# Odd mixer of a two-block transformer kernel: attention values as two float32r passes per head, softmax division moved to ScalarE, query and key tiles projected pair by pair

## The chip, the cores and the metric

The kernel runs on one core of a Trainium2 chip. The metric is the device time of one execution in microseconds. The kernel before was run three times; its median is 1922.75 us (1922.05 to 1923.62).

## What is computed

The reference takes 512 tokens of width 1024 in float32 through two blocks: a differential attention with a mixture of experts, and then an even mixer, a gated FFN, an odd mixer, a second FFN and a last norm. The change is almost all in the odd mixer:

```python
def odd_mixer(xn, w_in, w_out, forget_b, sinks, rope_h):
    qc, kc, vc, fc, qd, kd, vd = _split(xn @ w_in, ODD_SPLITS)
    log_f = jax.nn.log_sigmoid(fc + forget_b)
    yc = forgetting_attention(heads(qc, 8), heads(kc, 8), heads(vc, 8), log_f)
    yd = sink_window_gqa(apply_rope(heads(qd, 8)), apply_rope(heads(kd, 2)), heads(vd, 2), sinks)
    return jnp.concatenate([yc, yd], -1) @ w_out
```

`forgetting_attention` is causal softmax attention with 8 heads of 64, whose logits get the difference of a cumulated log forget gate. `sink_window_gqa` lets each block of 128 queries see its own and the previous block, with 8 query heads on 2 value heads, and a learned sink in the denominator.

## The kernel before, in words

The whole program stands in one class with a method per stage; the odd mixer is `stage_e` (L937 to L1118). All matrices lie in 128 partitions. A weight product in near-full precision is three float32r matmuls: `split` makes a high part on ScalarE (L110) and a low part on VectorE (L111), and `mm3` issues high by high, high by low and low by high (L135 to L137, or L139 to L141 where the activations are the stationary operand). In profile and order, these are `mm<-...`. `fm` makes a projection with tokens along the free axis, `tm` one with tokens on the partitions.

`stage_e` first projects part 1 of the values (`v_units(1)`, 324 columns), then `kd` and four tiles `qd` with rotary embedding, and then runs two series of heads, four query blocks each:

- **window heads** (`w_score`, `w_turn`, `w_value`): scores `s` (two passes), bias and minimum on VectorE (L1065), Exp on ScalarE (L1067), Exp of the sink (L1068), sum and reciprocal, division on VectorE (L1071), transposes `t` on TensorE (L1080), two copies from PSUM on ScalarE (L1083, L1084), values `pv` (L1095).
- **forgetting heads** (`soft_heads`, L681 on, shared with the even mixer): scores (L694), bias and minimum (L697), Exp (L698), reciprocal (L699), division (L700), transposes (L709), one copy of the turned block (L711), and at a head's last block its four value matmuls (L721).

The value matmuls take float32 on both sides: 64 columns of values are stationary, the turned weights move. Two heads write the two halves of one PSUM bank, and `y_out` (L740) splits the bank into high and low for the output projection (L743, L744). PSUM holds four banks for `mm`, two for `s` (`ns`), one for `t` (`ntp`) and one for `pv` (`npv`).

A unit of the window series issues the score of a block, the turn of the block two before and the value of the one four before. `weave` sets these units between those of a projection: the window heads beside `qc`, `kc` and part 0 of the values, the forgetting heads beside the second half of the output projection (`mm<-ydh`, `mm<-ydl`). The first half (`mm<-ych`, `mm<-ycl`) follows. `prep(c)` makes stacked high and low parts of the queries and keys of heads 2c and 2c+1 (`nh`, `nl`, then about a dozen DMAs on SP's queue), and is asked for two heads ahead. The tile framework's scheduler then sets the order on each engine.

Of the kernel before, what the change touches and what calls it, by code (L numbers as in the profile page):

```python
# [23 lines left out]
SOFT, ATT, WIN = (2, 4), (1, 4), (2, 4)  # L24
# [57 lines left out]
class K:  # L82
# [598 lines left out]
    def soft_heads(self, pool, heads, begin):  # L681


        nc = self.nc
        sbs, pts, pvs = {}, {}, {}

        def score(u, i):
            hd = heads[u]
            if i == 0:
# [12 lines left out]
        def turn(u, i):  # L702
            n = P * (i + 1)
            if i == 0:
                pts[u] = pool.tile([P, 13, P], F32, name="ptall", tag="ptall", bufs=2)
# [5 lines left out]
            nc.scalar.copy(pts[u][:, i:4 * i + 1:3], tp[:, :n].rearrange("p (a b) -> p a b", b=P))  # L711

        def value(u, i):
            if i != NT - 1:
                return
            e = u % 2
            if e == 0:
                pvs[u // 2] = self.pvt()
            pv, pt = pvs[u // 2], pts.pop(u)
            for j in range(NT):  # L720
                nc.tensor.matmul(pv[64 * e:64 * e + 64, j * P:], lhsT=heads[u]["v"](j), rhs=pt[:, 4 * j:3 * j + 4],  # L721
                                 start=j == 0, stop=j == NT - 1, skip_group_check=True)
            if e == 1:
                heads[u]["done"](u // 2, pvs.pop(u // 2))

        us = [(u, i) for u in range(len(heads)) for i in range(NT)]
        units = []
        for t in range(len(us) + SOFT[1]):
            parts = [(f, us[t - d], c) for f, d, c in ((score, 0, 0.11), (turn, SOFT[0], 0.11), (value, SOFT[1], 0.3))
                     if 0 <= t - d < len(us)]  # L730

            def fn(parts=parts, t=t):
                if t == 0:
                    begin()
# [3 lines left out]
        return units  # L738

# [8 lines left out]
    def stage_c(self):  # L748
# [4 lines left out]
        with tc.tile_pool(name="pc", bufs=1) as pc:  # L753
# [167 lines left out]
            def head(kind, hh, v, begin, bias, y):  # L921
                def qk(i, n):
                    q, *k = stacks[kind, hh]
                    return [(q[:, i * P:(i + 1) * P], t[:, :n]) for t in k]
                return {"qk": qk, "bias": bias, "v": lambda j: v[:, j, hh * 64:hh * 64 + 64], "begin": begin, "done": self.y_out(y)}

            rel = self.soft_heads(pc, [head("b", hh, vb, rel_bias(hh), lambda i, n, hh=hh: mbs[hh][:, T - n:T], yb)
                                       for hh in range(8)], lambda: yb.extend([self.x8("ybh"), self.x8("ybl")]))
# [4 lines left out]
                                       for hh in range(8)], lambda: ya.extend([self.x8("yah"), self.x8("yal")]))  # L933
# [4 lines left out]
    def stage_e(self):  # L938
# [3 lines left out]
        self.nsb, self.nst, self.nsl = 4, 4, 2  # L942
        with tc.tile_pool(name="pe", bufs=1) as pe:
# [9 lines left out]
            vc = pe.tile([P, NT, 512], F32, name="vc")  # L953
            vd = pe.tile([P, NT, 128], F32, name="vd")
# [12 lines left out]
            def v_raw(part, k):  # L967
                r = self.wp.tile([P, 2048], F32, name="wr", tag="wr", bufs=self.nr)
                r = r[:, :4 * 324].rearrange("p (a b) -> p a b", a=4)
                if part == 0:  # L970
                    nc.sync.dma_start(r, wv[:, k:k + 4, 1024:1348])
                else:
                    nc.sync.dma_start(r[:, :, 0:196], wv[:, k:k + 4, 1348:1544])
                    nc.sync.dma_start(r[:, :, 196:324], wv[:, k:k + 4, 2184:2312])
                return r

            def d0(i, ps):
                nc.scalar.activation(vc[:, i, 0:324], ps, AF.Copy, scale=self.rt[:, i:i + 1])

            def d1(i, ps):  # L980
                rt = self.rt[:, i:i + 1]
                nc.scalar.activation(fz[:, i], ps[:, 188:196], AF.Copy, scale=rt)
                nc.scalar.activation(vd[:, i], ps[:, 196:324], AF.Copy, scale=rt)
                nc.scalar.activation(vc[:, i, 324:512], ps[:, 0:188], AF.Copy, scale=rt)
# [3 lines left out]
            def qk_tile(name, c0, n, scale):  # L988
                def done(m, ps):
                    t = pe.tile([P, T], F32, name=name, tag="qk", bufs=8)  # L990
# [4 lines left out]
                    if (name, m) == ("kc", 0):  # L995
                        self.after(2, lambda: prep(0))
                return self.fm(w[:, c0:c0 + n], x, done)
# [14 lines left out]
            v_units = lambda part, d: self.tm([(k, k + 4, (lambda k=k: v_raw(part, k))) for k in (0, 4)], 324, x, d)  # L1012
# [27 lines left out]
            self.emit(qk_tile("kd", 2056, 128, 1.0) + qk_tile("qd", 1544, 512, -0.125))  # L1040
            self.flush()
# [5 lines left out]
            prep_window(0)  # L1047


            yd, yc, sbs, pts, pvs = [], [], {}, {}, {}  # L1050

            def w_score(hh, i):
                if hh == 0 and i == 0:
                    yd.extend([self.x8("ydh"), self.x8("ydl")])
                if i == 0 and hh % 2 == 0 and hh < 6:
                    prep_window(hh // 2 + 1)
# [7 lines left out]
                st = pe.tile([P, 4], F32, name="stw", tag="stw", bufs=6)  # L1064
# [6 lines left out]
                nc.vector.tensor_scalar(sb[:, :n], sb[:, :n], st[:, 3:4], None, op0=OP.mult)  # L1071

            def w_turn(hh, i):
                n = P if i == 0 else 2 * P
                if i == 0:
                    pts[hh] = pe.tile([P, NT, 256], F32, name="ptw", tag="ptall", bufs=2)
                sb, pt = sbs.pop((hh, i)), pts[hh]
# [4 lines left out]
                if i:  # L1082
                    nc.scalar.copy(pt[:, i - 1, P:2 * P], tp[:, 0:P])  # L1083
                nc.scalar.copy(pt[:, i, 0:P], tp[:, n - P:n])  # L1084

            def w_value(hh, i):
                if i != NT - 1:
                    return
                c, e, g = hh // 2, hh % 2, hh // 4
                if e == 0:  # L1090
                    pvs[c] = self.pvt()
                pv, pt = pvs[c], pts.pop(hh)
                for j in range(NT):
                    m = min(2, NT - j) * P
                    nc.tensor.matmul(pv[64 * e:64 * e + 64, j * P:j * P + m], lhsT=vd[:, j, g * 64:g * 64 + 64],  # L1095
                                     rhs=pt[:, j, :m], start=j == 0, stop=j == NT - 1, skip_group_check=True)
                if e == 1:
                    self.y_out(yd)(c, pvs.pop(c))

            us = [(hh, i) for hh in range(8) for i in range(NT)]  # L1100
            window = []
            for t in range(len(us) + WIN[1]):
                parts = [(f, us[t - d]) for f, d in ((w_score, 0), (w_turn, WIN[0]), (w_value, WIN[1])) if 0 <= t - d < len(us)]
# [8 lines left out]
            heads = [{"qk": lambda i, n, hh=hh: [(q[:, i * P:(i + 1) * P], k[:, :n]) for q, k in stacks[hh]],  # L1112
                      "bias": lambda i, n: cm[:, T - n:T], "v": lambda j, hh=hh: vc[:, j, hh * 64:hh * 64 + 64],
                      "begin": lambda hh=hh: prep(hh // 2 + 1) if hh % 2 == 0 and hh < 6 else None,
                      "done": self.y_out(yc)} for hh in range(8)]
            forg = self.soft_heads(pe, heads, lambda: yc.extend([self.x8("ych"), self.x8("ycl")]))
            self.emit(self.weave(forg, self.fm(w_out[512:1024], lambda k: (yd[0][:, k], yd[1][:, k]), self.add_h), tail=1))
            self.emit(self.fm(w_out[0:512], lambda k: (yc[0][:, k], yc[1][:, k]), self.last_add))  # L1118
# [606 lines left out]
```

## Time and profile before

| | before |
|---|---|
| median of 3 runs | 1922.75 us (1922.05 to 1923.62) |
| profiled execution | 1921.22 us |
| its span | 1919.5 us |
| TensorE busy | 1841.3 us (96%) |
| VectorE busy | 1321.3 us (69%) |
| ScalarE busy | 975.1 us (51%) |
| GpSimd busy | 227.3 us (12%) |

The profiled execution lies 1.7 us above its own span and 1.5 us below the median. PE is TensorE's matmuls, PEld its weight loads, DVE VectorE, ACT ScalarE, POOL GpSimd, SP the engine that issues most DMAs. Times inside the program are microseconds from the start of the span. In it the odd mixer's part from the forget sums to the next norm runs from 1343.7 to 1542.3, the window heads from about 1388 to 1451 and the forgetting heads to about 1515.

### The profile page before, as it was taken

How to read it: one execution, taken by the hardware profiler on the slowest of the kernel's cores; microseconds unless marked ns; L12 is line 12 of the kernel's file. 1: busy time of each engine (PE TensorE's matmuls, PEld its weight loads, DVE VectorE, ACT ScalarE, POOL GpSimd, SP SyncE). 2: the span in 40 equal slices, each digit the busy share in tenths (PEclk: the TensorE clock that was granted, in tenths of full speed). 3: DMA queues.
4: the chain of work that ended last, by engine and by line, in shares of the span. 5: the costliest groups of instructions: out<-in, count | busy, mean ns of one | idle time of the engine just before them, and what ended most of it. 6: DMA issues, size and time to landing. Idle time of an engine off the chain costs nothing.

```text
span 1919.5 us, 24632 instructions
## 1 busy us (share of the span) xinstructions
PE 1841.3 (96%) x8604; PEld 1451.1 (76%) x8605; DVE 1321.3 (69%) x2817; ACT 975.1 (51%) x1660; POOL 227.3 (12%) x281
## 2 busy tenths in 40 slices
PE   8999996999998999998999999999999999999997
PEld 6767585778887877675688888887877788888885
DVE  6586757999997779855677447744476677637753
ACT  5565554888885424436554224434276544324442
POOL 2000012222221301310200000012200100000001
PEclk9999897999999999999999999999999999999998
DMA  5521047999995454445233343334545233243331
GB/s 189 180 67 56 33 159 239 345 372 365 370 374 202 123 136 116 113 135 133 68 91 93 86 114 92 86 90 136 140 115 130 57 102 92 83 118 93 85 87 59
DMA packets 260098, 274.74 MB, mean 143 GB/s; under 512 B 14438, under 2 KB 175622, under 8 KB 259968
## 3 DMA queue, kind: packets, MB, share of 16 engines
q1 hardware_dynamic: 250688, 257.56, 43.8%
q0 software_dynamic: 5072, 10.00, 1.5%
q10 hardware_dynamic: 4208, 5.56, 0.8%
q8 instruction: 69, 1.13, 0.2%
q14 instruction: 61, 0.50, 0.1%
HBM read 238.19 MB, written 15.73 MB: 132 GB/s over the span
## 4 chain that ended last, share of the span: by engine, by line
PE 56%; DVE 7%; DMA 2%; ACT 2%; issue 1%; POOL 1%; SPq 0%; DVEq 0%; ACTq 0%; POOLq 0%
PE mm L135 15%; PE mm L137 15%; PE mm L136 15%; PE pv L721 2%; PE t L709 1%; DVE wl L111 1%; DVE sc L884 1%; DVE m L883 1%; PE mm L139 1%; PE mm L140 1%; PE mm L141 1%; PE s L694 1%; PE pv L1095 1%; DVE sb L697 1%; ACT sb L698 0%
## 5 line engine op out<-in xcount | busy, mean ns | idle before, releaser
L110 ACT CAST wh<-wr 128x1024 fp32r<-128x1024 f32 (+5 forms) x335 | 306.7, 916 | 440.6 <-PE mm L136 322.1
L111 DVE TENSOR_TENSOR wl<-wr,wh 128x1024 fp32r<-128x1024 f32 (+4 forms) x332 | 356.2, 1076 | 201.0 <-ACT wh L110 198.3
L135 PE MATMUL mm<-xh,wh 128*128 128x512 f32 x952 | 372.5, 391 | 2.0 <-DVE h L378 1.8
L137 PE MATMUL mm<-xh,wl 128*128 128x512 f32 x952 | 372.2, 391 | 0.2 <-DVE wl L111 0.2
L136 PE MATMUL mm<-xl,wh 128*128 128x512 f32 x952 | 371.3, 390 | 0.0
L135 PEld LDWEIGHTS mm<-xh,wh 128*128 128x128 f32 x952 | 178.8, 188 | 39.7 <-issue 3.5
L137 PEld LDWEIGHTS mm<-xh,wl 128*128 128x128 f32 x952 | 178.8, 188 | 37.9 <-issue 1.1
L136 PEld LDWEIGHTS mm<-xl,wh 128*128 128x128 f32 x952 | 178.8, 188 | 36.3 <-issue 0.2
L111 DVE TENSOR_TENSOR wl<-wx,wh 128x1024 fp32r<-128x1024 f32 x123 | 151.8, 1252 | 11.8 <-ACT wh L110 5.8
L110 ACT CAST wh<-wx 128x1024 fp32r<-128x1024 f32 x134 | 139.5, 1051 | 29.3 <-PE mm L141 24.4
L139 PE MATMUL mm<-wh,xh 128*128 128x512 f32 (+2 forms) x352 | 131.8, 378 | 9.7 <-ACT wh L110 5.6
L135 PE MATMUL mm<-hh,wh 128*128 128x512 f32 x352 | 138.9, 395 | 0.0
L136 PE MATMUL mm<-hl,wh 128*128 128x512 f32 x352 | 138.9, 395 | 0.0
L137 PE MATMUL mm<-hh,wl 128*128 128x512 f32 x352 | 138.9, 395 | 0.0
L140 PE MATMUL mm<-wl,xh 128*128 128x512 f32 (+2 forms) x352 | 130.0, 370 | 3.4 <-DVE wl L111 3.4
L141 PE MATMUL mm<-wh,xl 128*128 128x512 f32 (+2 forms) x352 | 129.0, 367 | 0.0
L618 DVE TENSOR_TENSOR z<-mm,rb 128x512 f32<-128x512 f32 x88 | 60.4, 688 | 81.0 <-PE mm L137 81.0
L139 PE MATMUL mm<-wh,xeh 128*128 128x512 f32 x256 | 103.8, 406 | 0.8 <-ACT xeh L1356 0.8
L277 POOL TENSOR_TENSOR acc<-acc,sq 128x512 f32<-128x512 f32 x42 | 58.1, 1383 | 387.6 <-ACT sq L273 387.2
L141 PE MATMUL mm<-wh,xel 128*128 128x512 f32 x256 | 101.6, 397 | 0.0
L140 PE MATMUL mm<-wl,xeh 128*128 128x512 f32 x256 | 101.2, 395 | 0.0
L378 DVE TENSOR_TENSOR h<-mm,h 128x512 f32<-128x512 f32 x88 | 60.5, 690 | 52.1 <-PE mm L137 50.9
(412 smaller groups left out, 3365.2 us busy)
## 6 DMA issues: line engine op xcount, KB each, us to landing
wr<-in_ffn_w_up SPq DMA_DIRECT2D x88, 512.0 KB, 4.9
wx<-in_moe_w_gate SPq DMA_DIRECT2D x23, 1024.0 KB, 9.4
wx<-in_moe_w_up SPq DMA_DIRECT2D x22, 1024.0 KB, 8.2
wx<-in_moe_w_down SPq DMA_DIRECT2D x22, 1024.0 KB, 9.9
wr<-in_ffn_w_down SPq DMA_DIRECT2D x32, 704.0 KB, 4.6
wr<-in_da_w_in SPq DMA_DIRECT2D x11, 1024.0 KB, 5.2
wr<-in_even_w_in SPq DMA_DIRECT2D x11, 1024.0 KB, 5.6
wr<-in_moe_w_up SPq DMA_DIRECT2D x10, 1024.0 KB, 8.4
```

The costliest lines, as they stand in the source:

```text
L110: nc.scalar.copy(h, raw)
L111: (nc.gpsimd if eng else nc.vector).tensor_tensor(l, raw, h.bitcast(F32), op=OP.subtract)
L135: mm(out, lhsT=wh, rhs=xh, start=first, stop=False, skip_group_check=True)
L136: mm(out, lhsT=wh, rhs=xl, start=False, stop=False, skip_group_check=True)
L137: mm(out, lhsT=wl, rhs=xh, start=False, stop=last, skip_group_check=True)
L139: mm(out, lhsT=xh, rhs=wh, start=first, stop=False, skip_group_check=True)
L140: mm(out, lhsT=xh, rhs=wl, start=False, stop=False, skip_group_check=True)
L141: mm(out, lhsT=xl, rhs=wh, start=False, stop=last, skip_group_check=True)
L277: nc.gpsimd.tensor_tensor(self.acc, self.acc, sq, op=OP.add)
L378: self.nc.vector.tensor_tensor(self.h[:, m], ps, self.h[:, m], op=OP.add)
L618: nc.vector.tensor_tensor(z[:, 2:], ps, self.rb, op=OP.mult)
L721: nc.tensor.matmul(pv[64 * e:64 * e + 64, j * P:], lhsT=heads[u]["v"](j), rhs=pt[:, 4 * j:3 * j + 4], start=j == 0, stop=j == NT - 1, skip ...
```

## The change

- **Values.** `vc` and `vd` hold, per head, 64 columns of high and 64 of low parts (`heads_hl`). The turned weights are split on leaving PSUM (`pt_put`): high by a cast on ScalarE, low by VectorE, which reads the same bank and the high part. Each float32 value matmul becomes two float32r ones with a stationary operand of 128 by 128: first the high weights (`pth`, `pwh`), then the low ones (`ptl`, `pwl`). The two halves of the result are added in `y_join` (a ScalarE copy of 64 partitions, a VectorE add), and the output's high and low parts come from that sum.
- **Division.** A ScalarE Copy with a per-row scale takes the place of VectorE's multiplication, one unit after the score (`norm`, `w_norm`).
- **Order.** Blocks run from 3 down to 0, value stands before turn, the lags are 1, 2, 3. The even mixer's heads keep their division and their lags; only value and turn swap there.
- **Projections.** `qk_tile` makes one tile of 128 columns. Pair 0 and 1 and part 0 of the values lie beside the window heads, pair 2 and 3 and then the second half of the output projection beside the forgetting heads. Value parts have 256 and 392 columns instead of 324 and 324. `prep` is asked for one head ahead; `qs` and `kh` have three buffers instead of four.

```diff
 def value(u, i):
+    if "v2" in hd:
+        pv = self.pvt()
+        for j in range(NT):
+            for m, t in enumerate(pt):
+                nc.tensor.matmul(pv[:, j * P:], lhsT=hd["v2"](j), rhs=t[:, 4 * j:3 * j + 4], start=j + m == 0,
+                                 stop=j == NT - 1 and m == 1, skip_group_check=True)
+        self.y_join(pool, u, pv, hd["done"])
+        return
...
+def pt_put(self, to, tp):
+    nc.scalar.copy(to[0], tp)
+    if len(to) == 2:
+        nc.vector.tensor_tensor(to[1], tp, to[0].bitcast(F32), op=OP.subtract)
+def y_join(self, pool, u, pv, done):
+    e = u % 2
+    if e == 0:
+        self.yj = [pool.tile([P, T], F32, name=n, tag=t, bufs=1) for n, t in zip(("yj", "yk"), self.join_tags)]
+    a, b = self.yj
+    own, other = self.half(e), self.half(1 - e)
+    nc.scalar.copy(a[own], pv[other])
+    nc.vector.tensor_tensor(b[own], pv[own], a[own], op=OP.add)
+    if e == 1:
+        done(u // 2, b)
...
-            nc.vector.tensor_scalar(sb[:, :n], sb[:, :n], st[:, 2:3], None, op0=OP.mult)
+            if one is None:
+                nc.vector.tensor_scalar(sb[:, :n], sb[:, :n], st[:, 2:3], None, op0=OP.mult)
+        def norm(u, i):
+            sb, st = sbs[u, i][:, :P * (i + 1)], sts.pop((u, i))
+            nc.scalar.activation(sb, sb, AF.Copy, scale=st[:, 2:3])
...
-        self.nsb, self.nst, self.nsl = 4, 4, 2
+        self.nsb, self.nst, self.nsl = 4, 3, 2
...
+            def heads_hl(to, ps, rt):
+                ps = ps.rearrange("p (a b) -> p a b", b=64)
+                nc.scalar.activation(to[:, :, 0:64], ps, AF.Copy, scale=rt)
+                nc.vector.scalar_tensor_tensor(to[:, :, 64:128], ps, rt, to[:, :, 0:64].bitcast(F32), op0=OP.mult, op1=OP.subtract)
...
-            proj = qk_tile("qc", 0, 512, -0.125) + qk_tile("kc", 512, 512, 1.0) + v_units(0, d0)
-            self.emit(proj[:2])
-            self.emit(self.weave(window, proj[2:]))
+            first = pair(0) + v_units(0, d0) + pair(1)
+            self.emit(self.weave(window, first))
...
-            self.emit(self.weave(forg, self.fm(w_out[512:1024], lambda k: (yd[0][:, k], yd[1][:, k]), self.add_h), tail=1))
-            self.emit(self.fm(w_out[0:512], lambda k: (yc[0][:, k], yc[1][:, k]), self.last_add))
+            beside(8, pair(2))
+            beside(8, pair(3))
+            out = self.fm(w_out[512:1024], lambda k: (yd[0][:, k], yd[1][:, k]), self.add_h)
+            beside(8, out[:3])
+            beside(8, out[3:6])
+            beside(len(forg), out[6:])
+            self.emit(self.fm(w_out[0:512], lambda k: yc[k], self.last_add))
```

TensorE at the last forgetting head, before. `t` are the transposes, `pv` the value matmuls, `mm<-ydh` and `mm<-ydl` the second half of the output projection, `mm<-ych` the first:

```order
L709 MATMUL t<-ident,sb 128x128 x4
L135 MATMUL mm<-ydh,wh 128x512
L136 MATMUL mm<-ydl,wh 128x512
L137 MATMUL mm<-ydh,wl 128x512
L135 MATMUL mm<-ydh,wh 128x512
L721 MATMUL pv<-ptall,vc 64x512
L721 MATMUL pv<-ptall,vc 64x384
L721 MATMUL pv<-ptall,vc 64x256
L721 MATMUL pv<-ptall,vc 64x128
L136 MATMUL mm<-ydl,wh 128x512
L137 MATMUL mm<-ydh,wl 128x512
```

The same place after the change, from the transposes of the last head on (`mm<-yc` reads the last two heads' output):

```order
L718 MATMUL t<-ident,sb 128x128 x10
L731 MATMUL pv<-pth,vc 128x512
L731 MATMUL pv<-ptl,vc 128x512
L731 MATMUL pv<-pth,vc 128x384
L731 MATMUL pv<-ptl,vc 128x384
L731 MATMUL pv<-pth,vc 128x256
L731 MATMUL pv<-ptl,vc 128x256
L731 MATMUL pv<-pth,vc 128x128
L731 MATMUL pv<-ptl,vc 128x128
L135 MATMUL mm<-yc,wh 128x512 x2
L136 MATMUL mm<-yc,wh 128x512
L137 MATMUL mm<-yc,wl 128x512
```

Before, matmuls of the second half stand between and behind the last head's work; after, all ten transposes and the eight value passes of the last head stand together, and the next matmul reads their result. Counted in the full order: between the value passes of heads 4 and 5 no projection matmul is left, between those of heads 5 and 6 six, between those of 6 and 7 none; heads 0 and 4 have 14 each, heads 1 to 3 from 21 to 23.

TensorE one head earlier in the change, between the value passes of heads 4 and 5, where the order holds transposes and scores alone:

```order
L731 MATMUL pv<-ptl,vc 128x128
L718 MATMUL t<-ident,sb 128x128 x4
L697 MATMUL s<-k_12834,q_12830 128x384
L697 MATMUL s<-kh,qs 128x256
L697 MATMUL s<-k_12834,q_12830 128x256
L718 MATMUL t<-ident,sb 128x128 x3
L697 MATMUL s<-kh,qs 128x128
L697 MATMUL s<-k_12834,q_12830 128x128
L718 MATMUL t<-ident,sb 128x128 x2
```

The four groups of transposes use the one bank of `t` in turn, with at most three score passes between two groups.

ScalarE in a late forgetting head after the change (`pth` is the cast of a turned block, L701 Exp, L709 the division, L777 the copy of `y_join`):

```order
L765 CAST pth<-t 128x4x128
L701 ACTIVATE sb,st<-sb,st 128x512
L1178 CAST yc<-yk 128x512
L709 ACTIVATE sb<-sb,st 128x512
L765 CAST pth<-t 128x3x128
L701 ACTIVATE sb,st<-sb,st 128x384
L709 ACTIVATE sb<-sb,st 128x384
L765 CAST pth<-t 128x2x128
```

Before, the same place held one copy and one Exp for each block; now a division stands between the casts as well.

## Rows read from the trace of the kernel before

**Rows 1.** The page's first part: busy time of each engine, share of the span.

```profile
PE 1841.3 (96%) x8604; PEld 1451.1 (76%) x8605; DVE 1321.3 (69%) x2817; ACT 975.1 (51%) x1660; POOL 227.3 (12%) x281
```

**Rows 2.** Windows: length, then busy PE, PEld, DVE, ACT, POOL; clock, DMA share.

```profile
1388.00:1451.00 63.00, 62.40 (x348) 47.22 (x348) 43.71 (x181) 45.89 (x172) 0.00 (x0) 1.00 0.50 130
1451.00:1515.00 64.00, 64.00 (x310) 43.09 (x309) 43.19 (x152) 41.65 (x114) 1.24 (x5) 1.00 0.37 90
```

**Rows 3.** Windows of the tile pv alone: PE, PEld, DVE, ACT.

```profile
1388.00:1451.00 63.00, 15.37 (x64) 7.44 (x64) 2.06 (x3) 1.75 (x3) 1.00 0.50 130
1451.00:1515.00 64.00, 19.96 (x66) 7.77 (x64) 3.44 (x5) 2.93 (x5) 1.00 0.37 90
```

**Rows 4.** Timeline of PE: value matmuls of two heads, and what follows (start, length).

```profile
1416.57 1.73 PE L1095 MATMUL pv<-ptw,vd 128*64 128x256 f32 x8
...
1418.23 0.33 PE L1061 MATMUL s<-kh,qs 128*128 128x128 f32 x1
...
1510.75 2.37 PE L721 MATMUL pv<-ptall,vc 128*64 128x512 f32 x8
...
1513.05 0.50 PE L136 MATMUL mm<-ydl,wh 128*128 128x512 f32 x1
```

**Rows 5.** Timeline of PE: neighbouring float32r passes of 512, 256 and 324 columns.

```profile
1510.19 0.39 PE L137 MATMUL mm<-ydh,wl 128*128 128x512 f32 x1
...
1510.42 0.40 PE L135 MATMUL mm<-ydh,wh 128*128 128x512 f32 x1
...
1389.04 0.28 PE L1061 MATMUL s<-kl,qs 128*128 128x256 f32 x1
...
1389.16 0.40 PE L135 MATMUL mm<-xh,wh 128*128 128x512 f32 x1
...
1327.93 0.31 PE L140 MATMUL mm<-wl,xh 128*128 128x324 f32 x1
...
1328.08 0.31 PE L141 MATMUL mm<-wh,xl 128*128 128x324 f32 x1
```

**Rows 6.** Timeline of PE in part 1 of the value projection: one wait.

```profile
1322.74 0.42 PE L140 MATMUL mm<-wl,xh 128*128 128x324 f32 x1 [0.93 <-DVE wl L111]
```

**Rows 7.** Groups by form, 1388 to 1515: count, busy, mean ns, idle before.

```profile
L697 DVE CUSTOM_DVE_ANT_0 sb<-s,cm 128x384 f32<-128x384 f32 x8 | 4.4, 549 | 0.2 <-PE s L694 0.2
...
L711 ACT COPY ptall<-t 128x512 f32<-128x512 f32 x8 | 4.6, 579 | 0.8 <-PE t L709 0.8
...
L700 DVE TENSOR_SCALAR sb<-sb,st 128x512 f32<-128x512 f32 x8 | 3.9, 485 | 0.2
...
L711 ACT COPY ptall<-t 128x384 f32<-128x384 f32 x8 | 3.8, 475 | 2.9 <-PE t L709 2.6
...
L744 DVE TENSOR_TENSOR ycl<-pv,ych 128x512 fp32r<-128x512 f32 x4 | 2.8, 689 | 5.3 <-ACT ych L743 5.3
...
L743 ACT CAST ych<-pv 128x512 fp32r<-128x512 f32 x4 | 2.3, 586 | 5.8 <-PE pv L721 5.8
```

**Rows 8.** Timeline: four transposes, their copy, and the next ScalarE instruction.

```profile
1478.64 0.66 PE L709 MATMUL t<-ident,sb 128*128 128x128 f32 x4
...
1479.39 0.56 ACT L711 COPY ptall<-t 128x512 f32<-128x512 f32 x1
...
1479.85 0.62 ACT L698 ACTIVATE sb<-sb,st 128x384 f32<-128x384 f32 x1
```

**Rows 9.** Windows in which the granted clock falls (columns as in rows 2).

```profile
192.00:193.00 1.00, 0.30 (x1) 0.14 (x1) 1.00 (x8) 0.30 (x3) 0.00 (x0) 1.00 1.03 401
...
195.00:207.50 12.50, 12.50 (x29) 7.20 (x30) 6.14 (x31) 4.77 (x18) 0.00 (x0) 0.50 0.07 27
...
635.00:637.50 2.50, 2.50 (x11) 2.50 (x12) 2.50 (x2) 0.92 (x2) 2.48 (x4) 0.50 1.08 373
```

**Rows 10.** Timeline of SP's queue: first and last DMA of one `prep`.

```profile
1455.78 0.54 SPq L661 DMA_DIRECT2D qs<-nh  x1
...
1466.99 1.17 SPq L1009 DMA_DIRECT2D k<-fhl  x2
```

More of the change, by code (lines that the diff above doesn't have):

```diff
@@ L22 @@
 SKIP = 4096
-SOFT, ATT, WIN = (2, 4), (1, 4), (2, 4)
+ATT = (1, 4)
 _CST = {}
@@ L679, in k_stack, with soft_heads @@
         return out
-    def soft_heads(self, pool, heads, begin):
+    def soft_heads(self, pool, heads, lags):
         nc = self.nc
-        sbs, pts, pvs = {}, {}, {}
+        one, two, three = lags
+        sbs, sts, pts, pvs = {}, {}, {}, {}
         def score(u, i):
             hd = heads[u]
-            if i == 0:
+            if i == hd["order"][0]:
                 hd["begin"]()
@@ L709, in turn, with fn @@
                 nc.tensor.transpose(tp[:, j * P:(j + 1) * P], sb[:, j * P:(j + 1) * P], self.ident)
-            nc.scalar.copy(pts[u][:, i:4 * i + 1:3], tp[:, :n].rearrange("p (a b) -> p a b", b=P))
+            self.pt_put([t[:, i:4 * i + 1:3] for t in pts[u]], tp[:, :n].rearrange("p (a b) -> p a b", b=P))
         def value(u, i):
-            if i != NT - 1:
+            hd = heads[u]
+            if i != hd["order"][-1]:
                 return
-            e = u % 2
+            e, pt = u % 2, pts.pop(u)
+            if "v2" in hd:
[6 more added lines that the diff above has]
+                return
             if e == 0:
                 pvs[u // 2] = self.pvt()
-            pv, pt = pvs[u // 2], pts.pop(u)
+            pv = pvs[u // 2]
             for j in range(NT):
-                nc.tensor.matmul(pv[64 * e:64 * e + 64, j * P:], lhsT=heads[u]["v"](j), rhs=pt[:, 4 * j:3 * j + 4],
+                nc.tensor.matmul(pv[64 * e:64 * e + 64, j * P:], lhsT=hd["v"](j), rhs=pt[0][:, 4 * j:3 * j + 4],
                                  start=j == 0, stop=j == NT - 1, skip_group_check=True)
             if e == 1:
-                heads[u]["done"](u // 2, pvs.pop(u // 2))
-        us = [(u, i) for u in range(len(heads)) for i in range(NT)]
+                hd["done"](u // 2, pvs.pop(u // 2))
+        us = [(u, i) for u in range(len(heads)) for i in heads[u]["order"]]
         units = []
[L728 to L734, printed above, removed]
+        for t in range(len(us) + three):
+            parts = [(f, us[t - d], c) for f, d, c in ((score, 0, 0.11), (norm, one, 0.0), (value, three, 0.3), (turn, two, 0.11))
+                     if d is not None and 0 <= t - d < len(us)]
+            def fn(parts=parts):
                 for f, u, _ in parts:
@@ L738, in soft_heads, with pt_tiles @@
         return units
+    def pt_tiles(self, pool, two):
+        if not two:
+            return [pool.tile([P, 13, P], F32, name="ptall", tag="ptall", bufs=2)]
+        return [pool.tile([P, 13, P], F32R, name=n, tag="ptall", bufs=2) for n in ("pth", "ptl")]
+    def pt_put(self, to, tp):
+        nc = self.nc
+        nc.scalar.copy(to[0], tp)
+        if len(to) == 2:
+            nc.vector.tensor_tensor(to[1], tp, to[0].bitcast(F32), op=OP.subtract)
+    def y_join(self, pool, u, pv, done):
+        nc = self.nc
+        e = u % 2
[7 more added lines that the diff above has]
+            done(u // 2, b)
     def y_out(self, y):
@@ L1010, in prep @@
                     stacks[2 * c + e] = (q[e], k[e][0]), (q2[n + e], k2[n + e])
-            v_units = lambda part, d: self.tm([(k, k + 4, (lambda k=k: v_raw(part, k))) for k in (0, 4)], 324, x, d)
+            v_units = lambda part, d: self.tm([(k, k + 4, (lambda k=k: v_raw(part, k))) for k in (0, 4)], 392 if part else 256, x, d)
             fhl = pe.tile([40, T], F32R, name="fhl")
@@ L1047, in stage_e @@
             prep_window(0)
-            yd, yc, sbs, pts, pvs = [], [], {}, {}, {}
+            self.emit(qk_tile("qd", 2, 1544, -0.125) + qk_tile("qd", 3, 1544, -0.125))
+            yd, yc, rest, sbs, sts, pts = [], [], [], {}, {}, {}
             def w_score(hh, i):
[L1053 to L1056, printed above, removed]
+                if i == NT - 1 and hh % 2:
+                    prep_window(hh // 2 + 1) if hh < 6 else prep(0)
                 lo = max(0, i - 1) * P
@@ new lines, in f_done @@
+            def f_done(c, y):
+                if c < 2:
+                    h, l = (pe.tile([P, T], F32R, name=n, tag="qk", bufs=6) for n in ("ych", "ycl"))
+                else:
+                    rest.extend([self.x8("yc")] if c == 2 else [])
+                    h, l = rest[0][:, 2 * c - 4], rest[0][:, 2 * c - 3]
+                nc.scalar.copy(h, y)
+                nc.vector.tensor_tensor(l, y, h.bitcast(F32), op=OP.subtract)
+                yc.append((h, l))
+            forg = self.soft_heads(pe, [{"qk": lambda i, n, hh=hh: [(q[:, i * P:(i + 1) * P], k[:, :n]) for q, k in stacks[hh]],
+                                         "bias": lambda i, n: cm[:, T - n:T], "v2": lambda j, hh=hh: vc[:, j, hh],
+                                         "begin": lambda hh=hh: begin(hh), "done": f_done, "order": (3, 2, 1, 0)}
+                                        for hh in range(8)], (1, 2, 3))
```

105 lines of the change are left out of this document (57 added, 48 removed).

## The prediction

> **What bounds the kernel now.** I read the page's busy times first: TensorE works 96% of the span [rows 1], so it is the bound almost everywhere. Then I cut out the stretch that the change rewrites, window heads and forgetting heads, and asked each engine for its time there. TensorE is busy 62.4 of 63 us and then 64 of 64 us, VectorE 43.7 and 43.2, ScalarE 45.9 and 41.7 [rows 2]. The reader is to see that TensorE never waits there for long, and that the other two have about 40 us of room each. So work taken off TensorE is worth its full time, as long as something else stands ready for it. The order of instructions tells where that fails.
>
> **The value matmuls (gain).** In the two windows they are busy 15.37 and 19.96 us, 35.3 together [rows 3], but fragments that wait or overlap are in that. Dense, the eight instructions of a window head take 1418.23 - 1416.57 = 1.66 us to the next start and those of a forgetting head 1513.05 - 1510.75 = 2.30 [rows 4]: 8 x (1.66 + 2.30) = 31.7 us. The new passes are priced by the starts of neighbouring float32r passes: 0.23 us at 512 columns, 0.12 at 256, 0.15 at 324 [rows 5]. For 384 I take 0.18, between its neighbours. For 128 I take that of 256 as an upper bound. A window head then costs 8 x 0.12 = 0.96 us, a forgetting head 2 x (0.23 + 0.18 + 0.12 + 0.12) = 1.30; eight of each are 18.1 us. The saving lies between 31.7 - 18.1 = 13.6 and 35.3 - 18.1 = 17.2; I take the middle, 15.4, since both dense and fragmented heads occur.
>
> FP8 and Floating Point Precision (the Trainium skill, section TensorE Precision Notes) says that true FP32 takes four passes through the array. By that alone two passes save half of the 31.7 us, an estimate of 15.9, within the bounds of the rows.
>
> **Value projection.** 96 passes of 324 columns become 256 wide (-0.03 us each, -2.9) and 96 become 392 wide (+0.03, +2.9) [rows 5]. One wait of 0.93 us for a low part stands in the wide half [rows 6]; longer passes may cover it. Between 0 and -0.9; I take -0.5.
>
> **The division, the low parts and the join (on other engines).** VectorE loses 8 divisions of 0.485 us at 512 columns and their smaller kin [rows 7]: about 12 us in the forgetting heads, and about 11 in the window heads by the same rate. It gains the low part of each turned block, like L744 at 0.689 us per 512 columns from PSUM, about 15 and 12 us, and 16 additions of that size, 11 us. That is +15 on 87 us. ScalarE gains the divisions at no more than the 0.586 us of a 512 cast [rows 7], about 13 and 11 us, and 16 copies, 9 us; it loses about 4 where two copies become one cast. That is about +29 on 88. So about 102 and 117 of 127 us by full durations: below TensorE on average, and I charge nothing for the totals. What is charged are the places where TensorE has nothing left beside them.
>
> **The tail of the forgetting heads (loss).** Here the order decides. The filler runs out early: no projection pass remains between the values of heads 4 and 5, six in head 6's turn, none in head 7's. Before, 32 passes of the second half and all of the first stood behind or between. So for heads 5, 6 and 7 TensorE runs at the pace of the turn. There is one PSUM bank for transposes, and it now has two readers in a row: the cast, and then the low part, which needs both the bank and the cast. For 512 columns: transposes 0.66, 0.09 until the cast starts [rows 8], cast 0.58, low part 0.69 [rows 7], and two more hand-overs of 0.09: 2.10 us. For 384: 0.50 + 0.475 + 0.55 + 0.27 = 1.80 [rows 7, 8]. In the same steps I take 1.40 for 256 and 1.05 for 128. The sum is 6.35 us, and the value passes of 1.30 stand behind the last low part: 7.65 us a head, 23.0 for three. Then the first matmul of the first half waits for the join: copy 0.59, addition 0.69, cast 0.59 and three hand-overs, 2.1 us [rows 7, 8]. That makes 25.1 us. TensorE's own work in it, by the same prices (1.1 transposes, 1.3 scores, 1.3 values per head, six passes), is 3.7 + 4.3 + 2.4 = 10.4. The loss is 14.7 us.
>
> **Smaller losses.** Heads 0 and 4 hold 14 filler passes: 14 x 0.23 + 3.7 = 6.9 us against a turn of 7.65, twice 0.75 = 1.5. Heads 1 to 3 with 21 or more have 8.5 us of work and lose nothing. The window heads now start with nothing projected ahead; bounds 0 and 2 us, I take 1.0.
>
> **Stacks one head ahead.** One preparation holds SP's queue from 1455.78 to 1468.2 [rows 10], longer than a head of 8 us, and a head's scores wait for its last rows. In the order the scores of heads 2, 4 and 6 stand about a head behind the first casts, so between 0 and 2 us each. I take 0 because the first head's stacks are issued in the first half of the queue's work; 6 us stay as an end. Value and turn changing places in the even mixer cost nothing: the same instructions, behind the same lags.
>
> **The clock.** The tail leaves TensorE about 10.4 of 25 us of work. In the trace the granted clock falls from 1.00 to 0.50 (2.4 to 1.2 GHz) soon after 192, where the emptiest microsecond still held a matmul for 0.30 of it, and stays there for the 12.5 us of 195 to 207.5; at 635 it is back after 2.5 [rows 9]. I expect the fall here. Behind the tail, the passes then take double for 2.5 to 12.5 us, which costs 1.3 to 6.3; inside it, transposes and value passes (2.4 us a head) sit on the turn's path and double, up to 2.5 heads or 6 us. Bounds 1.3 and 12.3; I take 5, near the lower third, since one of the two rows returns quickly.
>
> TensorE: Matmul & The Clock Gate (the Trainium skill, section on the HAM clock gate) lets the clock fall after an idle window. By that rule alone TensorE, which has work in almost every microsecond of the tail, keeps its clock and the case without a fall below holds; the row at 192 speaks against it.
>
> **Sum.** Gains 15.4 + 0.5 = 15.9; losses 14.7 + 1.5 + 1.0 = 17.2; clock 5. That is +6.3 us on the profiled execution's 1921.22: 1927.5. Its median of runs stands 1.5 higher, so I set 1929.
>
> **The rivals.**
> *Without the fall.* The same sum with the clock at 1.00 throughout: 1922.75 + 1.3 = 1924.0. For it: the gaps are short and regular. It would be no change, which I take as within 0.2%, about 3.9 us, as far as a measurement of this kernel can tell.
> *Faster: the turn overlaps.* Durations overstate what a buffer is held for: the copy of 0.56 us at 1479.39 is followed by the next ScalarE instruction after 0.46 [rows 8]. If each hand-over comes about 0.1 us before the recorded end, a head's turn is about 5.3 us, three heads and the join take 3 x 6.6 + 1.7 = 21.5, and the loss is 11.1; heads 0 and 4 then lose nothing. With the saving at its upper end, 17.2 + 0.9, and no fall, the time is 1922.75 - 18.1 + 11.1 = 1915.8. It decides from a mean turn under about 1.3 us a block. Against it: the low part must wait for a cast that is truly finished.
> *The two passes are no cheaper than one old one,* because loading 128 columns sets the pace. At 256 columns the starts lie 0.12 us apart with such loads [rows 5], so only the 128-column passes can be held up; I give it nothing of its own.
>
> **How the numbers follow.** The fall 0.45, with a range of its own of 1925 to 1937; no change 0.30; faster 0.25. The fall makes it slower in nearly all of its range. The predicted time is 1929. The range goes from 1914, just under the faster case, to 1937, which takes in the clock's upper bound or late stacks of 6 us, not both.
>
> **What would show it.** Right: the tile pv busy near 18 to 20 us in the two windows; behind head 4's values, four groups of transposes per head about 1.6 us apart, with TensorE waiting for VectorE's low part (L767); a granted clock of 0.50 about there; then a wait of about 2 us for the cast of `yc`. Wrong: a busy share of TensorE above 0.7 in the last three heads, or TensorE waiting for stacks at heads 2, 4 and 6, or ScalarE busy without a pause through heads 1 to 3.

## The result, and the profile after

The change makes the kernel slower: 1934.96 us median (1932.06 to 1938.0, five runs) against 1922.75 (1919.91 to 1925.02, five runs by now), a ratio of 1.0065 with a 95% interval of 1.0051 to 1.0079. The profiled execution of the changed kernel has a span of 1931.8 us, 12.3 more than before.

The page's busy times, to be read against [rows 1]:

```profile
PE 1839.1 (95%) x8604; PEld 1456.2 (75%) x8605; DVE 1343.6 (70%) x2843; ACT 1010.1 (52%) x1714; POOL 226.7 (12%) x281
```

TensorE is busy 2 us less, though the execution is 12 longer: the work that was taken away came back as waits and as work at half the clock. Windows of the changed kernel show where: window heads 1 to 7, forgetting heads 0 to 4, heads 5 to 7 up to the first matmul on their result, and the rest up to the next norm. Columns are those of [rows 2].

```profile
1385.72:1452.05 66.33, 64.07 (x354) 49.99 (x354) 50.88 (x170) 55.97 (x166) 2.63 (x2) 1.00 0.51 133
1452.05:1497.73 45.68, 43.16 (x224) 32.36 (x224) 38.66 (x110) 40.29 (x102) 0.00 (x0) 1.00 0.53 134
1497.73:1529.13 31.40, 19.26 (x76) 13.88 (x75) 14.01 (x42) 17.74 (x42) 0.00 (x0) 0.72 0.00 1
1529.13:1555.96 26.83, 25.66 (x103) 20.06 (x104) 18.44 (x25) 15.38 (x24) 9.60 (x11) 0.94 0.40 111
```

The difference of length and busy time is TensorE's waiting: 2.3, 2.5, 12.1 and 1.2 us. Before, it was 0.6 us over all sixteen heads [rows 2] and 0.9 in the rest, so the first three stretches are what is new. The third stretch is the tail: three heads take 31.4 us, TensorE is busy for 19.3 of it, and at a mean granted clock of 0.72 part of that is stretched work. VectorE and ScalarE are busy for 14.0 and 17.7 us there: no engine is full. It is a chain.

The timeline of the changed kernel's last head shows the chain (start, length, engine, line, instruction, wait before it and its releaser):

```profile
1518.15 0.63 PE L718 MATMUL t<-ident,sb 128*128 128x128 f32 x4
1518.35 0.58 ACT L777 COPY yj<-pv 64x512 f32<-64x512 f32 x1 [0.65 <-PE pv L731]
1518.96 0.59 ACT L765 CAST pth<-t 128x512 fp32r<-128x512 f32 x1
1518.97 0.68 DVE L778 TENSOR_TENSOR yk<-pv,yj 64x512 f32<-64x512 f32 x1 [1.70 <-ACT yj L777]
1519.58 0.69 DVE L767 TENSOR_TENSOR ptl<-t,pth 128x512 fp32r<-128x512 f32 x1
...
1520.33 0.55 PE L718 MATMUL t<-ident,sb 128*128 128x128 f32 x3 [1.54 <-DVE ptl L767]
1520.91 0.48 ACT L765 CAST pth<-t 128x384 fp32r<-128x384 f32 x1 [1.36 <-PE t L718]
1521.42 0.56 DVE L767 TENSOR_TENSOR ptl<-t,pth 128x384 fp32r<-128x384 f32 x1 [1.15 <-ACT pth L765]
...
1522.03 0.69 PE L718 MATMUL t<-ident,sb 128*128 128x128 f32 x2 [1.16 <-DVE ptl L767]
...
1524.47 0.80 PE L731 MATMUL pv<-pth,vc 128*128 128x512 f32 x1 [0.35 <-ACT pth L765]
...
1525.06 0.63 PE L731 MATMUL pv<-ptl,vc 128*128 128x512 f32 x1
...
1525.49 0.53 PE L731 MATMUL pv<-pth,vc 128*128 128x384 f32 x1
...
1528.46 0.62 ACT L1178 CAST yc<-yk 128x512 fp32r<-128x512 f32 x1 [0.76 <-DVE yk L778]
...
1529.13 0.80 PE L135 MATMUL mm<-yc,wh 128*128 128x512 f32 x1 [2.04 <-ACT yc L1178]
```

Transposes, cast, low part, then the next transposes; each engine waits for the one before it. Also to be seen is what the prediction left out: the join of the head before (L777, L778) stands ahead of the first cast and the first low part. The second value pass of 512 columns starts 0.43 us before its successor here, where a pass of that width took 0.23 [rows 5]: the clock has fallen by then.

### The profile page after: what moved, and what is told of

Same layout as the page of the kernel before. It is cut to its first block, busy times and chain, and to the rows that moved or that the text cites. A ratio compares the mean times of both kernels' runs of the same rounds, so it can differ in the third digit from the quotient of the medians.

```text
span 1931.8 us, 24727 instructions
## 1 busy us (share of the span) xinstructions
PE 1839.1 (95%) x8604; PEld 1456.2 (75%) x8605; DVE 1343.6 (70%) x2843; ACT 1010.1 (52%) x1714; POOL 226.7 (12%) x281
## 4 chain that ended last, share of the span: by engine, by line
PE 54%; DVE 8%; ACT 3%; issue 1%; DMA 1%; POOL 1%; SPq 0%; DVEq 0%; ACTq 0%; POOLq 0%
PE mm L137 15%; PE mm L135 15%; PE mm L136 15%; PE pv L739 1%; DVE wl L111 1%; PE t L718 1%; DVE sc L926 1%; DVE m L925 1%; PE mm L139 1%; PE mm L140 1%; PE s L697 1%; PE mm L141 1%; PE pv L731 1%; DVE sb L700 1%; ACT wh L110 0%
## 5 line engine op out<-in xcount | busy, mean ns | idle before, releaser
L110 ACT CAST wh<-wr 128x1024 fp32r<-128x1024 f32 (+4 forms) x333 | 306.2, 921 | 423.8 <-PE mm L136 300.8
L111 DVE TENSOR_TENSOR wl<-wx,wh 128x1024 fp32r<-128x1024 f32 x123 | 151.3, 1247 | 12.2 <-ACT wh L110 5.8
L139 PE MATMUL mm<-wh,xh 128*128 128x512 f32 (+3 forms) x352 | 131.5, 376 | 9.6 <-ACT wh L110 5.6
L140 PE MATMUL mm<-wl,xh 128*128 128x512 f32 (+3 forms) x352 | 129.9, 369 | 2.5 <-DVE wl L111 2.5
L141 PE MATMUL mm<-wh,xl 128*128 128x512 f32 (+3 forms) x352 | 129.5, 368 | 0.0
```

Source lines behind the costliest of these rows:

```text
L110: nc.scalar.copy(h, raw)
L111: (nc.gpsimd if eng else nc.vector).tensor_tensor(l, raw, h.bitcast(F32), op=OP.subtract)
L139: mm(out, lhsT=xh, rhs=wh, start=first, stop=False, skip_group_check=True)
L140: mm(out, lhsT=xh, rhs=wl, start=False, stop=False, skip_group_check=True)
L141: mm(out, lhsT=xl, rhs=wh, start=False, stop=last, skip_group_check=True)
```

## The experiments

Twelve kernels were run, each against the kernel before on the same chip. Beside the ratio stands the length of the stretch from the forget sums to the next norm in the one profiled execution of each (from the first `pf` to the next `ss` on TensorE, 1341.5 to 1543.3 before), since the program ahead of it, the same in nearly all of them, began that stretch anywhere from 1340 to 1348 us.

| kernel | ratio to before (95%) | stretch, us |
|---|---|---|
| before | 1 | 201.9 |
| the change | 1.0065 (1.0051 to 1.0079) | 213.0 |
| three banks shared by scores and transposes | 0.9965 (0.9952 to 0.9978) | 194.8 |
| division on VectorE | 1.0046 (1.0031 to 1.0062) | 208.9 |
| no low part | 1.0024 (1.0011 to 1.0037) | 206.1 |
| old values | 1.0039 (1.0015 to 1.0063) | 209.3 |
| value tile among the projection's banks | 1.0117 (1.0088 to 1.0146) | 221.9 |
| two banks for transposes, one for scores | 0.9962 (0.9946 to 0.9979) | 191.8 |
| both kinds of sharing | 1.0099 (1.0063 to 1.0134) | 219.7 |
| three shared banks, division on VectorE | 1.0005 (0.9989 to 1.0021) | 203.4 |
| dummy transposes in the tail | 1.0061 (1.0044 to 1.0078) | 208.8 |
| old values, two banks for transposes | 1.0047 (1.0029 to 1.0066) | 214.9 |
| before, two banks for transposes | 1.0019 (1.0007 to 1.0031) | 205.1 |
| two banks for transposes, all qd first | 0.9998 (0.9985 to 1.0011) | 196.9 |

**More banks for the transposes.** Theory: one bank with two readers in a row sets the pace of a head that has nothing beside it. Rival: ScalarE's load does. The first kernel lets the transposes take any of three banks that they share with the scores:

```diff
-        self.nmm, self.ns, self.ntp, self.npv = 4, 2, 1, 1
+        self.nmm, self.ns, self.ntp, self.npv = 4, 3, 0, 1
-        return self.pp.tile([P, 512], F32, name=name, tag="t", bufs=self.ntp)
+        return self.pp.tile([P, 512], F32, name=name, tag="t" if self.ntp else "s", bufs=self.ntp or self.ns)
```

> Scores and transposes share three PSUM banks, where the change gives the scores two and the transposes one. If the one bank with two readers sets the pace of the late heads, the tail from the value passes of head 4 to the first matmul on yc falls from 31.4 us to 24 or less, the clock stays at 1.00 through most of it, and the time is 1918 to 1926 us. If ScalarE's load (the division at 0.72 us per 512 columns) sets the pace, the tail stays within 3 us and the time is 1931 or more.

Measured: 1915.97 us median, 2 below the range, ratio 0.9965. The tail of three heads takes 22.7 us (7.42, 7.15 and 8.15) instead of 31.4. The second kernel moves one bank from the scores to the transposes:

```diff
-        self.nmm, self.ns, self.ntp, self.npv = 4, 2, 1, 1
+        self.nmm, self.ns, self.ntp, self.npv = 4, 1, 2, 1
```

> Two banks for the transposes, one for the scores; the rest as in the change. By the bank theory the late heads turn faster, need fewer projection passes and keep 14 to 18 each: 1914 to 1922 us. If the scores' second bank was needed as much, the waits move to the scores and the time is 1925 or more.

Measured: 1912.47 us, 1.5 below the range, ratio 0.9962. Its windows, with the same stretches as those of the change above:

```profile
1383.80:1440.68 56.88, 52.59 (x296) 41.51 (x296) 46.73 (x163) 51.07 (x159) 3.52 (x2) 0.97 0.50 129
1440.68:1483.48 42.80, 42.01 (x226) 32.63 (x225) 35.59 (x111) 40.48 (x108) 0.00 (x0) 1.00 0.55 141
1483.48:1504.98 21.50, 21.36 (x118) 17.36 (x117) 17.96 (x51) 17.78 (x46) 0.00 (x0) 1.00 0.29 76
1504.98:1533.97 28.99, 28.11 (x122) 22.44 (x122) 19.23 (x27) 16.73 (x26) 9.06 (x11) 1.00 0.38 105
```

The tail is 21.5 us instead of 31.4 (up to the next matmul, which here need not be one on the last heads' result), TensorE waits 0.1 us in it, the clock is 1.00, and 122 matmuls are left for the rest instead of 103. In its order 13, 18 and 18 projection passes stand beside the three heads instead of 0, 6 and 0, although the program asks for them at the same places: heads that turn faster leave fewer gaps, so fewer passes are used up early. That order is set before the program runs, so the second bank acts in two ways at once, by a freer turn and by the passes that are left beside it; these two kernels don't tell the two apart. Both kernels beat the kernel before. The rival that ScalarE's load sets the pace falls: these kernels have the same ScalarE work as the change.

**Division back on VectorE.**

```diff
-                                        for hh in range(8)], (1, 2, 3))
+                                        for hh in range(8)], (None, 2, 3))
...
+                nc.vector.tensor_scalar(sb[:, :n], sb[:, :n], st[:, 3:4], None, op0=OP.mult)
...
-((w_score, 0), (w_norm, 1), (w_value, 3), (w_turn, 2))
+((w_score, 0), (w_value, 3), (w_turn, 2))
```

> The division goes back to VectorE in all heads of the odd mixer, the rest as in the change. By the bank theory the turn is no shorter, the tail stays at 28 to 32 us and the time is 1930 to 1937. By the ScalarE theory a late head loses 2.2 us of ScalarE, the tail is about 25 us and the time 1924 to 1928.

Measured: 1931.42 us, and the tail is 29.9 us, as the bank theory said. With the banks shared the same edit was run again:

> Three shared banks for scores and transposes as in the run before it of that kind (1916 us), and the division back on VectorE. If ScalarE's division of 0.72 us per 512 columns still costs on the heads' way, 1910 to 1914 us; if VectorE, with 23 us more, becomes the slower engine, 1918 to 1926.

Measured: 1923.8 us, ratio 1.0005, against 0.9965 with the division on ScalarE. The longest of TensorE's waits in its forgetting heads (waited for, us in total, times, longest):

```profile
PE t L718 <- DVE sb L704: 2.6, 4, 1.8
```

L704 is VectorE's division. VectorE is busy 42.2 of 43.9 us in heads 0 to 4. That is only part of it: the stretch is 8.6 us longer than with the division on ScalarE, and the forgetting heads up to the tail's end hold 2.8 of that; 5.3 stand ahead of them, where the window heads have VectorE's division too. So once the turn is free, the move of the division to ScalarE is worth 0.4%, about 8 us. With the single bank its return measured 0.2% less, which the two intervals don't tell from nothing.

**No low part, old values.** One reader less at the bank: the first leaves out the low part of the weights, the second has one cast and no join. The first one's edit, cut:

```diff
         nc.scalar.copy(to[0], tp)
-        if len(to) == 2:
-            nc.vector.tensor_tensor(to[1], tp, to[0].bitcast(F32), op=OP.subtract)
...
-                for m, t in enumerate(pt):
+                for m, t in enumerate(pt * 2):
```

> The low parts of the turned weights are left out (the second value pass reads the high part again, so TensorE does the same work); one reader holds the transposes' bank. By the bank theory each head's turn is 1.9 us shorter in the tail, 31.4 becomes 23 to 26 us, and the time is 1921 to 1928. By the ScalarE theory nothing changes: 1931 or more.

> The change with the float32 value matmuls of before: one cast of each turned block, two heads in one bank, no join; order, division on ScalarE and projections by pairs as in the change. If the loss comes from the split of the weights (second reader, join), this has 14 us more of TensorE work but no long tail: 1920 to 1928. If the division or the new order loses the time, it is slower than the change by up to 14 us: 1935 to 1948.

Measured: 1927.11 and 1932.85 us. The first lies in the range of the bank theory, but the trace shows more than the ranges asked for. Two stretches of the kernel without low part, one of its window heads and its last three heads:

```profile
1415.72:1447.05 31.33, 23.07 (x93) 17.55 (x92) 17.07 (x62) 25.25 (x80) 0.00 (x0) 0.58 0.27 60
...
1505.74:1524.18 18.44, 18.15 (x98) 14.68 (x98) 10.34 (x29) 13.73 (x36) 0.00 (x0) 1.00 0.21 58
```

One of the kernel with old values, and behind it all its forgetting heads:

```profile
1409.27:1444.01 34.74, 27.87 (x131) 17.63 (x131) 18.90 (x82) 28.18 (x97) 0.00 (x0) 0.90 0.31 70
...
1444.01:1526.08 82.07, 81.99 (x388) 57.41 (x387) 39.44 (x121) 56.85 (x146) 0.00 (x0) 1.00 0.47 126
```

The late heads wait for next to nothing now: 18.4 us without the low part, less than the 23 to 26 expected, since projection passes stand beside all three. But the window heads have used up their passes: in the order of the old values 4, 0, 0 and 6 stand beside window heads 4 to 7. TensorE waits 8.3 and 6.9 us in the window stretches of the two kernels and the clock falls in both. The second expectation fails on both sides: the time is lost without a long tail, in window heads that have run out of passes. Whether the new order or the division brings them there is not shown. With two banks for the transposes, old values do no better:

> The float32 value matmuls of before in the change's order, with two banks for transposes and one for scores. If the two passes are worth the 13.6 to 17.2 us that the rows gave once the turn no longer holds TensorE up, this is slower than the run with two banks and two passes (1912.5 us) by 10 to 17: 1922 to 1930. If TensorE's work was never the limit, it is within 4 us of it.

Measured: 1931.55 us, just above the range of times: 19 more than with two passes, or 16 by the two ratios, since the kernel before ran 1.6 us slower beside it. From 1409 to 1440, in the window heads, TensorE waits 6.7 us at a clock of 0.75, so this does not price the passes alone; that price stays with the rows ahead of the prediction.

**Passes held back.** If matmuls that are used up early are the whole loss, holding them back should cure it with the single bank:

```diff
-        self.nmm, self.ns, self.ntp, self.npv = 4, 2, 1, 1
+        self.nmm, self.ns, self.ntp, self.npv = 5, 2, 1, 0
-        return self.pp.tile([P, 512], F32, name=name, tag="pv", bufs=self.npv)
+        return self.pp.tile([P, 512], F32, name=name, tag="pv" if self.npv else "mm", bufs=self.npv or self.nmm)
```

> The value tile takes its bank from the projection's five instead of one of its own, so that projection tiles can't run far ahead of the heads: in the order 22, 14 and 34 projection passes stand beside heads 5, 6 and 7 instead of 0, 6 and 0. The transposes keep their single bank with two readers. If the loss comes from matmuls that were used up early, the clock stays at 1.00 there and the time is 1916 to 1924 us. If the bank itself sets every head's pace, it stays at 1930 or more.

> Scores and transposes share three banks, values and projections five. If bank and used-up matmuls are two separate losses, this gains more than either: 1910 to 1915 us. If they are one loss seen twice, it is within 3 us of the better one, 1914 to 1919.

Measured: 1943.63 and 1940.46 us. The first stays above 1930, as the single bank would have it, but not for that reason; the second misses both ranges. Windows of the first: the stretch up to the first window head's values, and the last three heads.

```profile
1343.75:1388.22 44.47, 33.75 (x138) 25.81 (x138) 23.44 (x53) 17.91 (x45) 11.20 (x9) 0.80 0.50 127
...
1508.33:1536.70 28.37, 27.15 (x144) 22.01 (x143) 20.13 (x56) 21.04 (x51) 0.00 (x0) 1.00 0.23 75
```

The tail's waits are cured with the single bank: 1.2 us in 28.4, at full clock. So the bank costs next to nothing as long as passes stand beside it. But 10.7 us of waiting stand at the start of the window heads, with the clock at 0.80. The longest of TensorE's waits there (us in total, times, longest) is for a stack of queries:

```profile
PE s L1112 <- DMA qs<-nl: 7.3, 1, 7.3
```

From part 1 of the values to the first window head's value matmuls 144 projection passes stand here, 233 in the change, where TensorE doesn't wait for this DMA. Where passes stand decides where TensorE waits; moving them exposed another wait instead of ending one. I did not try to hold them back from the forgetting heads alone.

**The clock.** The change with 72 transposes more, which nobody reads, in the tail's gaps:

```diff
+            if "v2" in heads[u] and u >= 5 and i < 3:
+                if i == 2:
+                    pvs[u] = self.pvt()
+                for j in range(8):
+                    nc.tensor.transpose(pvs[u][:, 0:P], sb[:, 0:P], self.ident)
...
-                pv = self.pvt()
+                pv = pvs.pop(u) if u in pvs else self.pvt()
```

> The change with 72 transposes more that nobody reads, 24 in each of heads 5 to 7, written into the value bank before it is needed; the projection passes beside each head stay as in the change. They are 7 us of TensorE work at full clock. If the clock's fall is part of the tail's cost, it now stays at 1.00 longer there and the time is 1928 to 1933 us although more is done. If the fall costs nothing beside the waits, it is the same or slower, 1934 to 1942.

Measured: 1933.77 us, which tells nothing from the change's 1934.96. The profile does: heads 0 to 4, the tail, and the rest.

```profile
1456.75:1502.44 45.69, 43.17 (x225) 32.38 (x224) 38.64 (x110) 40.28 (x102) 0.00 (x0) 1.00 0.54 134
1502.44:1530.06 27.62, 21.64 (x148) 17.38 (x147) 13.96 (x42) 17.23 (x42) 0.00 (x0) 1.00 0.00 1
1530.06:1556.75 26.69, 25.82 (x102) 19.94 (x103) 18.44 (x25) 15.30 (x24) 9.58 (x11) 0.94 0.41 114
```

Heads 0 to 4 take 45.69 us, in the change 45.68. Then 148 instructions instead of 76 take 27.62 us instead of 31.40, and the clock stays at 1.00. So holding the clock up is worth up to 3.8 us in the tail, shown by more work in less time. By heads, first the change, then the kernel with dummies:

```profile
1497.73:1508.28 10.55, 7.58 (x30) 5.53 (x29) 4.98 (x17) 6.91 (x17) 0.00 (x0) 0.68 0.00 0
1508.28:1518.15 9.87, 6.72 (x29) 4.89 (x30) 5.74 (x18) 7.35 (x18) 0.00 (x0) 0.82 0.01 2
1518.15:1529.13 10.98, 4.95 (x21) 3.47 (x20) 3.29 (x7) 3.48 (x7) 0.00 (x0) 0.68 0.00 0
...
1502.44:1511.30 8.86, 7.58 (x54) 6.20 (x53) 4.94 (x17) 6.61 (x17) 0.00 (x0) 1.00 0.01 2
1511.30:1520.46 9.16, 7.94 (x55) 6.27 (x54) 5.72 (x18) 7.13 (x18) 0.00 (x0) 1.00 0.00 0
1520.46:1530.06 9.60, 6.11 (x45) 4.91 (x44) 3.29 (x7) 3.48 (x7) 0.00 (x0) 1.00 0.00 0
```

In the last head the order is the same but for the dummies, and 1.4 us are gained there. In heads 5 and 6 (1.7 and 0.7) some scores and projection passes stand at another place in the order as well, so these two shares are not the clock's alone for certain. Behind the tail the clock is 0.94 in both and the rest is equal: with the dummies the fall comes later, at 0.50 from 1532 to 1534. The times of whole runs, whose intervals are some 3 us wide to either side, don't resolve it.

**Controls.** The second bank alone, in the kernel before, and an attempt at the next wait in the best kernel (the join's tiles lie on the rotation tables, and the first window head's join waits for the last rotation):

```diff
+            self.emit(qk_tile("qd", 2, 1544, -0.125) + qk_tile("qd", 3, 1544, -0.125))
             kds = self.k_stack(pe, QD.pop(("kd", 0)))
...
             prep_window(0)
-            self.emit(qk_tile("qd", 2, 1544, -0.125) + qk_tile("qd", 3, 1544, -0.125))
```

> The kernel before with two banks for transposes and one for scores, nothing else. TensorE hardly waited there, so no change: within 0.2% of before. If the second bank alone brings what the run with two banks and two passes gained, it is 1912 to 1916.

> Two banks for transposes, and all four qd tiles projected before the first window stack, so that the join, whose two tiles lie on the rotation tables, needn't wait for the last rotation. If that wait (1.7 us of TensorE at the first window head) is all, 1909 to 1912 us; if the later start of the heads leaves them without projection passes at the end (two beside the last head in the order), 1914 to 1920.

Measured: 1925.41 us, ratio 1.0019, for the first: no gain, at the edge of no change. The bank helps only where the turn is on the path. The second is at 1921.36 us, just above its second range, ratio 0.9998, slower than without the edit. The wait for the join is gone, but TensorE waits 2.5 us for VectorE to take a key tile out of PSUM (L1044) instead, and its last head waits again, with two passes beside it (busy 3.59 of 7.18 us).

```profile
1504.62:1511.80 7.18, 3.59 (x21) 2.45 (x20) 3.64 (x10) 4.17 (x10) 0.00 (x0) 1.00 0.00 0
```

## Why the prediction was right, and where its sizes were off

The forecast was slower, +6.3 us, by the tail and the clock; measured are +12.2. Sign and place hold. The mechanism holds as it was summed in the last head, and in heads 5 and 6 other work of VectorE comes on top; the sum is half of what came. Of the 12.3 us by which the profiled execution is longer, 11.1 lie in the stretch of the table and 1.5 ahead of it.

- **Value matmuls.** The passes have the predicted pace at full clock: 0.24 us at 512 columns, 0.18 at 384 and 0.12 at 256, as the starts of head 1's passes at 1469.12, 1469.36, 1469.54, 1469.71 and 1469.83 show. The tile's busy time is 9.04 + 14.93 = 24.0 us in the two windows below, where 18 to 20 was expected: single passes with gaps between them count longer, and part of the second row ran at half clock. By busy time that saves 11.3 us instead of the 15.4 taken; no run prices the saving by itself. Columns as in [rows 3].

```profile
1385.72:1452.05 66.33, 9.04 (x58) 7.70 (x57) 4.80 (x7) 4.08 (x7) 1.00 0.51 133
1452.05:1529.13 77.08, 14.93 (x66) 12.59 (x65) 6.19 (x9) 5.23 (x9) 0.89 0.32 79
```

- **The tail.** The order gave its place exactly. 25.1 us were summed, 31.4 came, and 27.6 with the clock held up. (By its own terms the first block's 2.10 us should read 2.20, 0.3 us over three heads.) So the chain itself was 2.5 us short, and the rows by heads show where. Summed were 7.65 us a head and 2.1 behind the last. With the clock held up, the last head and the join take 9.60, where 9.75 was summed; heads 5 and 6 take 8.86 and 9.16. The sum holds where the turn stands alone, and is 1.2 and 1.5 us short in the two heads that also have the next head's scores. Head 6 of the change shows what stands in the way there:

```profile
1508.98 0.69 DVE L700 CUSTOM_DVE_ANT_0 sb<-s,cm 128x512 f32<-128x512 f32 x1 [3.08 <-PE t L718]
...
1509.12 0.59 ACT L765 CAST pth<-t 128x512 fp32r<-128x512 f32 x1
...
1509.71 0.69 DVE L778 TENSOR_TENSOR yk<-pv,yj 64x512 f32<-64x512 f32 x1
1510.44 0.69 DVE L767 TENSOR_TENSOR ptl<-t,pth 128x512 fp32r<-128x512 f32 x1
```

  The cast ends at 1509.71, but VectorE takes the next scores' bias and minimum (L700) and the join's addition (L778) first, and the low part starts 0.73 us later. In head 5 it is 0.49, in the last head 0.03. So the low part's wait, on which the sum rests, is the largest of TensorE's waits in the tail but a third of them, and most of it falls in the last head:

```profile
PE t L718 <- DVE ptl L767: 4.2, 4, 1.5
PE s L697 <- DVE st L700: 3.0, 5, 0.8
PE mm L135 <- ACT yc L1178: 2.0, 1, 2.0
PE t L718 <- DVE st L702: 1.8, 2, 1.0
PE pv L731 <- ACT pth L765: 1.1, 2, 0.7
```

  These are TensorE's waits in the tail of the change (us in total, times, longest). The wait for `yc`, predicted at 2.1 us, is 2.0.
- **The clock.** It fell where it was expected. 5 us were taken for it. Inside the tail 1.4 are shown in the last head, and up to 3.8 in all; behind it stand 26.83 us at a clock of 0.94, whose missing 0.06 is 1.6 us by estimate. The Trainium skill's rule (TensorE: Matmul & The Clock Gate, section on the HAM clock gate: a fall after an idle window) would by itself have kept the clock up. The trace disagrees: in the four microseconds around the fall TensorE was busy for 39 to 54% of each, and idle through none of them; the clock falls in the last:

```profile
1498.00:1499.00 1.00, 0.54 (x5) 0.28 (x3) 0.60 (x1) 0.97 (x2) 0.00 (x0) 1.00 0.00 0
1499.00:1500.00 1.00, 0.50 (x2) 0.30 (x2) 1.00 (x4) 0.94 (x3) 0.00 (x0) 1.00 0.00 0
1500.00:1501.00 1.00, 0.52 (x3) 0.31 (x3) 0.37 (x3) 0.61 (x1) 0.00 (x0) 1.00 0.00 0
1501.00:1502.00 1.00, 0.39 (x2) 0.39 (x2) 1.00 (x3) 0.89 (x3) 0.00 (x0) 0.78 0.00 0
```

- **Division.** ScalarE's took 0.724 us at 512 columns, not the 0.586 of a cast that was taken as its upper end; 0.485 was VectorE's [rows 7]. It was priced at nothing on the path, which is about right: with the single bank its return measured 0.2% less, within the intervals.
- **Smaller losses.** 2.5 us were taken for heads 0 and 4 and the windows' start. TensorE waits 2.3 us in window heads 1 to 7, 1.5 of them at head 1, and 2.5 in heads 0 to 4, 1.6 and 0.9 of them at heads 0 and 4: 4.8 together.
- **Value projection and stacks.** Part 1 took 19.26 us from its first to its last pass against 17.66 before, with its wait gone; part 0 was hidden in the heads. From 1385.7 on, no wait of TensorE for a DMA stands among its waits in either series of heads, so the price of 0 for late stacks holds.

Of the rivals, the faster one (a turn under 1.3 us a block) is excluded by the timeline: the 512 block takes 2.18 us from transposes to transposes, the 384 block 1.70. The case without the fall of the clock is what the run with dummy transposes shows for the tail: it is still 2.5 us longer than the 25.1 summed.

## What to carry to other kernels

When a result in PSUM gets a second reader, count how long its bank is held and what TensorE has beside it; a saving on TensorE turns into a wait as soon as the work beside a chain runs out. Read from the order where that work ends, and check a cure over the whole stretch: holding matmuls back exposed another wait and made the kernel slower, a second bank turned +0.65% into -0.4%. A stretch of the profile can resolve what medians of whole runs can't, as far as one execution of each goes.

## What was not expected of the hardware

- The clock falls in a stretch in which TensorE is busy for about half of the time and has work in every microsecond, and more work (148 instructions instead of 76) passes through the same three heads in 3.8 us less.
- A ScalarE Copy with a per-row scale from SBUF to SBUF takes 0.724 us per 512 columns, as long as the Exp beside it (0.724), while the cast from PSUM takes 0.587:

```profile
L701 ACT ACTIVATE sb<-sb,st 128x512 f32<-128x512 f32 x8 | 5.8, 724 | 0.0
L709 ACT ACTIVATE sb<-sb,st 128x512 f32<-128x512 f32 x8 | 5.8, 724 | 2.0 <-DVE st L702 1.9
...
L765 ACT CAST pth<-t 128x512 fp32r<-128x512 f32 x8 | 4.7, 587 | 0.2
```

  These are groups by form of the changed kernel (count, busy, mean ns, idle before).
